# Expert layer of a streaming-encoder block: index casts on another engine, a reduction over adjacent elements, and the last eight chunks' activations computed first

## The chip, the cores and the metric

The kernel runs on one core of a Trainium2 chip. The metric is the device time of one execution in microseconds. The time before the change is the median of three runs, 1779.57 us (1777.91 to 1783.63). The core's engines are TensorE (PE, matrix products), VectorE (DVE), ScalarE (ACT), GpSimd (POOL) and SyncE (SP, which here only issues DMAs). Each takes its instructions strictly in program order and waits on semaphores for the others, so an instruction that waits holds up everything behind it on its engine.

## The reference, cut to what matters

The block takes 512 tokens of 1024 channels. It computes chunked attention beside a diagonal state-space mixer, then cross-attention into 256 memory tokens, then an expert layer with 16384 single-neuron experts. The change touches only the expert layer:

```python
def _peer_ffn(hn, w_q, sub_keys, u_tab, v_tab):
    def block(xb):                                   # 128 tokens
        q = (xb @ w_q).reshape(PEER_BLOCK, PEER_HEADS, 2, PEER_QDIM // 2)
        s = jnp.einsum('thsd,hsnd->thsn', q, sub_keys).astype(jnp.float32)
        sv, si = lax.top_k(s, PEER_TOPK)             # 16 of 128, twice
        cand = (sv[:, :, 0, :, None] + sv[:, :, 1, None, :]).reshape(PEER_BLOCK, PEER_HEADS, -1)
        cidx = (si[:, :, 0, :, None] * PEER_KEYS + si[:, :, 1, None, :]).reshape(PEER_BLOCK, PEER_HEADS, -1)
        top, pos = lax.top_k(cand, PEER_TOPK)        # 16 of the 256 sums
        e = jnp.take_along_axis(cidx, pos, axis=-1)
        g = jax.nn.softmax(top, axis=-1)
        act = jax.nn.gelu(jnp.einsum('thkd,td->thk', u_tab[e], xb), approximate=False)
        w = (g * act).astype(xb.dtype)
        return jnp.einsum('thk,thkd->td', w, v_tab[e])
```

There are 8 heads, two key halves each, and 16 experts for each token and head.

## The kernel before

The 512 tokens are four blocks of 128. For one block (block 0) the expert rows are gathered from memory by index, 128 gathers from each table. For the other three blocks (384 tokens, `NT`) the kernel computes **all** 16384 experts densely, in 128 chunks of 128 experts, and multiplies the activations by a gate table that is zero where an expert was not chosen.

The expert layer has these stages.

1. *Queries and top-k.* `queries(h)` computes a head's scores on PE; ACT evacuates them (`pqT`, `sc`, `scl`). `topk(h, scs, g)` finds the 16 best on DVE: group 0 takes two token blocks, groups 1 and 2 one block each. It finds the best 16 of each half (`tv`, `ti`), casts the indices to floats and scales the first half's by 128 (`tf`, lines 890 and 891), adds 54 candidate pairs (`ca` on DVE, `cx` on POOL, line 898), finds the best 16 of those (`top`, `pi`), casts these positions to bf16 (`pf`, line 912), and picks the expert numbers out: `eq` on DVE compares a table of positions with `pf` (line 917), POOL multiplies `eq` by `cx` into `ev` (line 918), and DVE sums `ev` over the 54 candidates (line 919). `ev` has one buffer and is stored candidate by candidate, 16 numbers each, so the sum reads one element in 16. Group 0 of all heads and group 1 of heads 0 to 5 run in this stage.
2. *First U chunks.* A U chunk (`u_steps`) is one SP load of 512 KB (`wraw`), a split into a rounded half `whi` (ACT, line 108) and a rest `wlo` (line 110; POOL for the first `FREE` = 12 chunks, DVE for all later ones), 24 matmuls into `pa` (lines 124 to 126) and a Gelu on ACT into a tile `act` (line 1050). Chunks 0 to 11 are written behind the top-k.
3. *Gate table.* `build_w` makes the table in 48 quads of 8 tokens: DVE builds one-hot tables (`oAE`, line 1019, once; `oB`, line 1023, twice), PE multiplies them (`pw`, line 1028), ACT evacuates (`stg`, line 1031) and SP stores to `Wd` in memory. The generator yields 96 times, after every 8 `pw` matmuls. Between these steps stand the U chunks 12 to 27 (`FREE` to `LEAD` = 28), in pieces of 6 matmuls, and group 1 of heads 6 and 7.
4. *Main loop.* Iteration n computes U chunk n + 28 (while there is one) and V chunk n (`v_phase`): a load and a split of a V chunk, `act` times its gates `wt` (DVE, line 1074; `wt` is loaded from `Wd` by ACT's DMA queue), the split of the product (`ah` on ACT, line 1076, `al` on DVE, line 1080) and 18 matmuls into six accumulators `acc` (line 1084) that live through the whole loop. The 256 gathers (POOL) and their products (DVE) are spread over the iterations from n = 11 on; group 2 of the top-k stands in iterations 1 to 8. The last 28 iterations have V chunks only.

The order on each engine is made by a scheduler when the kernel is built, from the order of the code, the priorities that `tc.issue_after` sets, and a model of the instructions' lengths. The activations live in a ring of 31 tiles.

Of the kernel before, what the change touches and what calls it, by code (L numbers as in the profile page):

```python
# [800 lines left out]

NT = 384
LEAD = 28
FREE = 12
HOLD = 10
IOH = 2
ULV = (8,)
KS = 2
H0 = 2
SLACK = 4  # L810
# [9 lines left out]
def peer(tc, I, c, out):  # L820
# [5 lines left out]
    with tc.tile_pool(name="pp", bufs=1) as pp, tc.tile_pool(name="tq", bufs=2) as tq:  # L826
# [50 lines left out]
        def topk(h, scs, g):  # L877
            nb, b0 = len(scs[0]), (0, 2, 3)[g]
            tv = tq.tile([128, 2, nb, 16], F32, tag="tv", name="tv")
            ti = tq.tile([128, 2, nb, 16], U32, tag="ti", name="ti")  # L880
            for s in range(2):
                for b in range(nb):
                    sb = scs[s][b]
                    V.max(tv[:, s, b, 0:8], sb)
                    V.max_index(ti[:, s, b, 0:8], tv[:, s, b, 0:8], sb)
                    V.match_replace(sb, tv[:, s, b, 0:8], sb, NEG_BIG)
                    V.max(tv[:, s, b, 8:16], sb)
                    V.max_index(ti[:, s, b, 8:16], tv[:, s, b, 8:16], sb)
            tf = tq.tile([128, 2, nb, 16], F32, tag="tf", name="tf")
            V.tensor_copy(tf, ti)  # L890
            V.tensor_scalar(tf[:, 0], tf[:, 0], 128.0, None, op0=OP.mult)
            ca = tq.tile([128, nb, NC_], F32, tag="ca", name="ca")
            cx = tq.tile([128, nb, NC_], F32, tag="cx", name="cx")
            o = 0
            for i0, n, w_ in ROWS:
                for src, dst in ((tv, ca), (tf, cx)):
                    sh = [128, nb, n, w_]
                    (V if dst is ca else G).tensor_tensor(  # L898
                        dst[:, :, o:o + n * w_].rearrange("p b (n w) -> p b n w", n=n),
                        src[:, 0, :, i0:i0 + n].unsqueeze(3).broadcast_to(sh),  # L900
                        src[:, 1, :, 0:w_].unsqueeze(2).broadcast_to(sh), op=OP.add)
                o += n * w_
            pi = tq.tile([128, nb, 16], U32, tag="pi", name="pi")
            pf = tq.tile([128, nb, 16], BF16, tag="pf", name="pf")
            for b in range(nb):
                cb, tb = ca[:, b], top[:, b0 + b, h]
                V.max(tb[:, 0:8], cb)
                V.max_index(pi[:, b, 0:8], tb[:, 0:8], cb)
                V.match_replace(cb, tb[:, 0:8], cb, NEG_BIG)
                V.max(tb[:, 8:16], cb)  # L910
                V.max_index(pi[:, b, 8:16], tb[:, 8:16], cb)
            V.tensor_copy(pf, pi)
            for b in range(nb):
                sh = [128, NC_, 16]
                eq = tq.tile(sh, BF16, tag="eq", name="eq")
                ev = pp.tile(sh, F32, tag="ev", name="ev", bufs=1)
                V.tensor_tensor(eq, iob, pf[:, b].unsqueeze(1).broadcast_to(sh), op=OP.is_equal)
                G.tensor_tensor(ev, eq, cx[:, b].unsqueeze(2).broadcast_to(sh), op=OP.mult)
                V.tensor_reduce(ex[:, b0 + b, h], ev.rearrange("p n k -> p k n"), axis=AX.X, op=OP.add)  # L919

        def gates(g):
            r = ((0, 2), (2, 3), (3, 4))[g]
# [116 lines left out]
        acts = {}  # L1039
        wts = {}  # L1040

        def u_steps(n):
            w = load_split(I["ut"][n], G if n < FREE else V)
            pa = pst("s", "pa")[:, :NT]
            for k in range(8):
                mm3(pa, [t[:, k] for t in w], [PTh(k)[:, 128:], PTl(k)[:, 128:]], k == 0, k == 7)
                if k < 7 and (k + 1) % KS == 0:
                    yield
            acts[n] = act_tile("act")
            S.activation(acts[n], pa, AF.Gelu)  # L1050
            yield

        def u_phase(n):
            for _ in u_steps(n):
                pass
# [7 lines left out]
        def v_phase(n):  # L1063
# [13 lines left out]
            if n % 4 == WTP and n + 4 < 128:  # L1077
                with tc.issue_after(c.ah_ins):
                    load_wt(n // 4 + 1)
            c.v_ins = V.tensor_tensor(al, a, ah, op=OP.subtract).ins  # L1080
            for b in range(3):
                for (l, r) in ((ah, 0), (ah, 1), (al, 0)):
# [7 lines left out]
        prepare(1)  # L1090
        for n in range(FREE):
            u_phase(n)
        steps = (None for n in range(FREE, LEAD) for _ in u_steps(n))
        done = 0
        for q in range(96):
            next(gw)
            if q in LATE:
                i = LATE.index(q)
                with tc.issue_after(c.w_ins):
                    gates(1) if i == H0 else topk_late(8 - H0 + i, 1)  # L1100
            with tc.issue_after(c.pw_ins):
                while done < (q + 1) * (8 // KS) * (LEAD - FREE) // 96:
                    next(steps)
                    done += 1
        for _ in gw:
# [1 line left out]
        due = 0  # L1107
        res = []
        for n in range(128):
            if n + LEAD < 128:  # L1110
                u_phase(n + LEAD)
            v_phase(n)
            if 1 <= n < 9:
                with tc.issue_after(c.v_ins):
# [6 lines left out]
                        res.append(s8([128, 2, 1024], "res"))  # L1121
                        nc.scalar.dma_start(res[i][:, :2 - i], h2[1 + 2 * i:3 + i].rearrange("b p d -> p b d"))
            if n > HOLD:
                due += 256 * (2 if n + LEAD < 128 else 1) / (256 - LEAD - 2 * HOLD - SLACK)
            while due >= 1:
                due -= 1
                with tc.issue_after(c.split_ins):
# [78 lines left out]
```

## Time and profile before

| | |
|---|---|
| median of three runs | 1779.57 us |
| the profiled execution | 1780.63 us |
| its span, first to last instruction | 1778.9 us |
| mean granted PE clock | 0.977 |
| PE busy / DVE busy / ACT busy / POOL busy | 1682.0 / 1398.8 / 717.6 / 689.5 us |
| HBM read / written | 348.72 / 32.51 MB |

The page gives the busy time of each engine over the whole span and in 40 equal slices, the chain of work that ended last, and groups of instructions by line. Further views used below are the windows (one row for a stretch of time: busy time and instruction count of each engine, granted PE clock, DMA share and rate), the groups of one stretch kept apart by shape, the waits (who waited for whom: total, times, longest), and the timeline (start, length, engine, line, operation). A busy time of an instruction can cover the end of the one before it, since the engines pipeline; how far two instructions of one kind stand apart is read from their starts.

### The profile page before, as it was taken

How to read it: one execution, taken by the hardware profiler on the slowest of the kernel's cores; microseconds unless marked ns; L12 is line 12 of the kernel's file. 1: busy time of each engine (PE TensorE's matmuls, PEld its weight loads, DVE VectorE, ACT ScalarE, POOL GpSimd, SP SyncE). 2: the span in 40 equal slices, each digit the busy share in tenths (PEclk: the TensorE clock that was granted, in tenths of full speed). 3: DMA queues.
4: the chain of work that ended last, by engine and by line, in shares of the span. 5: the costliest groups of instructions: out<-in, count | busy, mean ns of one | idle time of the engine just before them, and what ended most of it. 6: DMA issues, size and time to landing. Idle time of an engine off the chain costs nothing.

```text
span 1778.9 us, 24797 instructions
## 1 busy us (share of the span) xinstructions
PE 1682.0 (95%) x8929; PEld 1462.1 (82%) x8929; DVE 1398.8 (79%) x2755; ACT 717.6 (40%) x1161; POOL 689.5 (39%) x566
## 2 busy tenths in 40 slices
PE   7898999999999668899999999999999999999999
PEld 6676778877788667788888999999999999999887
DVE  7998563644589999995998787777777877777886
ACT  4242573432333227785333333333333333333332
POOL 5432232341466651200345444444343434334451
PEclk9998999999999889999999999999999999999999
DMA  5412323220422226786449998888888888888895
GB/s 189 115 55 89 113 101 142 95 83 15 175 92 81 66 72 208 213 238 225 163 151 352 331 334 303 308 313 303 306 315 293 331 311 318 297 315 300 324 366 212
DMA packets 155820, 383.19 MB, mean 215 GB/s; under 512 B 13993, under 2 KB 70825, under 8 KB 155569
## 3 DMA queue, kind: packets, MB, share of 16 engines
q1 hardware_dynamic: 107504, 212.83, 35.1%
q0 software_dynamic: 36864, 134.23, 21.1%
q10 hardware_dynamic: 11328, 34.54, 5.5%
q8 instruction: 70, 1.15, 0.2%
q14 instruction: 54, 0.43, 0.1%
HBM read 348.72 MB, written 32.51 MB: 214 GB/s over the span
## 4 chain that ended last, share of the span: by engine, by line
PE 71%; DVE 22%; issue 3%; DMA 2%; POOL 1%; ACT 1%; SPq 0%; DVEq 0%; ACTq 0%; POOLq 0%
PE acc L1084 27%; PE pa L124 8%; PE pa L126 8%; PE pa L125 8%; PE pv L124 3%; PE pv L126 3%; PE pv L125 3%; DVE oB L1023 2%; DVE oAE L1019 2%; DVE ex L919 2%; DVE wlo L110 2%; PE pS L684 1%; PE po L694 1%; DVE ca L898 1%; PE pw L1028 1%
## 5 line engine op out<-in xcount | busy, mean ns | idle before, releaser
L108 ACT ACTIVATE whi<-wraw 128x1024 fp32r<-128x1024 f32 (+1 forms) x332 | 349.7, 1055 | 486.9 <-PE pa L125 229.9
L124 PE MATMUL pa<-PTh,whi 128*128 128x384 f32 x1024 | 355.8, 347 | 21.9 <-ACT act L1050 18.2
L126 PE MATMUL pa<-PTh,wlo 128*128 128x384 f32 x1024 | 350.5, 342 | 14.2 <-POOL wlo L110 10.8
L110 DVE TENSOR_TENSOR wlo<-wraw,whi 128x1024 fp32r<-128x1024 f32 x262 | 321.1, 1226 | 53.4 <-ACT whi L108 53.1
L125 PE MATMUL pa<-PTl,whi 128*128 128x384 f32 x1024 | 349.4, 341 | 0.0
L972 POOL DMA_INDIRECT vg<-in_peer_v_dram,ei x128 | 182.1, 1423 | 240.0 <-DVE X L973 216.7
L962 POOL DMA_INDIRECT ug<-in_peer_u_dram,ei x128 | 177.5, 1386 | 225.2 <-DVE ug L963 201.0
L1084 PE MATMUL acc<-wlo,ah 128*128 128x512 f32 x768 | 238.6, 392 | 0.8 <-DVE wlo L110 0.8
L1084 PE MATMUL acc<-whi,ah 128*128 128x512 f32 x768 | 239.2, 392 | 0.0
L1084 PE MATMUL acc<-whi,al 128*128 128x512 f32 x768 | 237.3, 391 | 0.0
L124 PEld LDWEIGHTS pa<-PTh,whi 128*128 128x128 f32 x1024 | 196.6, 192 | 28.1 <-ACT act L1050 20.3
L110 POOL TENSOR_TENSOR wlo<-wraw,whi 128x1024 fp32r<-128x1024 f32 x70 | 170.2, 2441 | 126.7 <-ACT whi L108 126.6
L126 PEld LDWEIGHTS pa<-PTh,wlo 128*128 128x128 f32 x1024 | 196.8, 192 | 17.2 <-POOL wlo L110 12.4
L125 PEld LDWEIGHTS pa<-PTl,whi 128*128 128x128 f32 x1024 | 196.7, 192 | 3.8
L973 DVE SCALAR_TENSOR_TENSOR X<-vg,dots,X 128x1024 f32<-128x1024 f32 x128 | 164.5, 1285 | 16.3 <-DMA vg<-in_peer_v_dram,ei 10.4
L1076 ACT ACTIVATE ah<-act 128x384 fp32r<-128x384 f32 x128 | 67.1, 526 | 260.7 <-PE acc L1084 241.5
L1084 PEld LDWEIGHTS acc<-wlo,ah 128*128 128x128 f32 x768 | 144.6, 188 | 33.3 <-DVE wlo L110 1.5
L1084 PEld LDWEIGHTS acc<-whi,al 128*128 128x128 f32 x768 | 144.1, 188 | 30.9
L963 DVE SCALAR_TENSOR_TENSOR ug<-ug,X 128x1024 f32<-128x1024 f32 x128 | 151.9, 1222 | 20.6 <-DMA ug<-in_peer_u_dram,ei 20.5
L1084 PEld LDWEIGHTS acc<-whi,ah 128*128 128x128 f32 x768 | 143.2, 188 | 23.7
L1080 DVE TENSOR_TENSOR al<-act,ah 128x384 fp32r<-128x384 f32 x128 | 70.9, 555 | 58.7 <-ACT ah L1076 56.3
L1074 DVE TENSOR_TENSOR act<-act,wt 128x384 f32<-128x384 f32 x128 | 66.0, 576 | 58.3 <-DMA wt<-Wd 58.3
(383 smaller groups left out, 2721.9 us busy)
## 6 DMA issues: line engine op xcount, KB each, us to landing
wraw<-in_ut_dram SPq DMA_DIRECT2D x128, 512.0 KB, 5.0
wraw<-in_peer_v_dram SPq DMA_DIRECT2D x128, 512.0 KB, 5.5
Wd<-stg SPq DMA_DIRECT2D x24, 1024.0 KB, 6.5
wt<-Wd ACTq DMA_DIRECT2D x32, 768.0 KB, 7.9
wraw<-in_w_pq_dram SPq DMA_DIRECT2D x16, 512.0 KB, 3.3
h<-in_x_dram SPq DMA_DIRECT2D x8, 512.0 KB, 7.2
wraw<-in_w_qk_dram SPq DMA_DIRECT2D x8, 512.0 KB, 3.7
wraw<-in_w_mk_dram SPq DMA_DIRECT2D x8, 512.0 KB, 3.3
```

The source lines that it names most:

```text
L108: S.activation(hi, raw, AF.Copy)
L110: ins = leng.tensor_tensor(lo, raw, hi, op=OP.subtract).ins
L124: P.matmul(out, lhs[0], rhs[0], start=first, stop=False)
L125: P.matmul(out, lhs[0], rhs[1], start=False, stop=False)
L126: P.matmul(out, lhs[1], rhs[0], start=False, stop=last)
L962: G.indirect_dma_start(out=ug, out_offset=None, in_=I["peer_u"], in_offset=IOX(ap=ei[:, k:k + 1], axis=0))
L963: V.scalar_tensor_tensor(ug, ug, 1.0, c.X0, op0=OP.mult, op1=OP.mult, accum_out=dots[:, k:k + 1])
L972: G.indirect_dma_start(out=vg, out_offset=None, in_=I["peer_v"], in_offset=IOX(ap=ei[:, k:k + 1], axis=0))
L973: V.scalar_tensor_tensor(a0, vg, dots[:, k:k + 1], a0, op0=OP.mult, op1=OP.add)
L1076: c.ah_ins = S.activation(ah, a, AF.Copy).ins
L1080: c.v_ins = V.tensor_tensor(al, a, ah, op=OP.subtract).ins
L1084: P.matmul(acc[b * 2 + d], l[:, b * 128:(b + 1) * 128], v[r][:, d * 512:(d + 1) * 512], start=n == 0 and l is ah and r == 0, stop=n == 127 ...
```

## The change

Three things are edited. The casts of the top-k indices and positions become ACT instructions. `ev` is stored the other way round, the 54 candidates of one result beside each other, so POOL writes with a stride and DVE's sum reads adjacent elements. And the U chunks are computed in another order: chunks 120 to 127 first (`NSPILL` = 8), then 0 to 119. The first eight activations are stored to memory (`Ad`) by ACT's DMA queue and loaded back by it in the iterations n = 117 to 124, three iterations ahead of their use. The gate table now has 24 U chunks spread over it (16 before), the main loop computes U chunk number n + 36 in its order, which is chunk n + 28, until n = 91, and the last 36 iterations have V chunks only.

```diff
 LEAD = 28
+NSPILL = 8
...
             tf = tq.tile([128, 2, nb, 16], F32, tag="tf", name="tf")
-            V.tensor_copy(tf, ti)
-            V.tensor_scalar(tf[:, 0], tf[:, 0], 128.0, None, op0=OP.mult)
+            S.activation(tf[:, 0], ti[:, 0], AF.Copy, scale=128.0)
+            S.activation(tf[:, 1], ti[:, 1], AF.Copy)
...
-            V.tensor_copy(pf, pi)
+            S.activation(pf, pi, AF.Copy)
             for b in range(nb):
                 sh = [128, NC_, 16]
                 eq = tq.tile(sh, BF16, tag="eq", name="eq")
-                ev = pp.tile(sh, F32, tag="ev", name="ev", bufs=1)
+                ev = pp.tile([128, 16, NC_], F32, tag="ev", name="ev", bufs=1)
                 V.tensor_tensor(eq, iob, pf[:, b].unsqueeze(1).broadcast_to(sh), op=OP.is_equal)
-                G.tensor_tensor(ev, eq, cx[:, b].unsqueeze(2).broadcast_to(sh), op=OP.mult)
-                V.tensor_reduce(ex[:, b0 + b, h], ev.rearrange("p n k -> p k n"), axis=AX.X, op=OP.add)
+                G.tensor_tensor(ev.rearrange("p k n -> p n k"), eq, cx[:, b].unsqueeze(2).broadcast_to(sh), op=OP.mult)
+                V.tensor_reduce(ex[:, b0 + b, h], ev, axis=AX.X, op=OP.add)
...
-        def u_steps(n):
-            w = load_split(I["ut"][n], G if n < FREE else V)
+        UORDER = [*range(128 - NSPILL, 128), *range(128 - NSPILL)]
+        Ad = c.dr.tile([NSPILL, 128, NT], F32, name="Ad")
+
+        def u_steps(j):
+            n = UORDER[j]
+            w = load_split(I["ut"][n], G if j < FREE else V)
...
-            acts[n] = act_tile("act")
-            S.activation(acts[n], pa, AF.Gelu)
+            a = act_tile("act")
+            S.activation(a, pa, AF.Gelu)
+            if j < NSPILL:
+                nc.scalar.dma_start(Ad[j], a)
+            else:
+                acts[n] = a
             yield
...
+            if 0 <= n + 3 - (128 - NSPILL) < NSPILL:
+                with tc.issue_after(c.ah_ins):
+                    acts[n + 3] = act_tile("act")
+                    nc.scalar.dma_start(acts[n + 3], Ad[n + 3 - (128 - NSPILL)])
...
-        steps = (None for n in range(FREE, LEAD) for _ in u_steps(n))
+        steps = (None for n in range(FREE, LEAD + NSPILL) for _ in u_steps(n))
...
-                while done < (q + 1) * (8 // KS) * (LEAD - FREE) // 96:
+                while done < (q + 1) * (8 // KS) * (LEAD + NSPILL - FREE) // 96:
...
-            if n + LEAD < 128:
-                u_phase(n + LEAD)
+            if n + LEAD + NSPILL < 128:
+                u_phase(n + LEAD + NSPILL)
...
-                due += 256 * (2 if n + LEAD < 128 else 1) / (256 - LEAD - 2 * HOLD - SLACK)
+                due += 256 * (2 if n + LEAD + NSPILL < 128 else 1) / (256 - LEAD - NSPILL - 2 * HOLD - SLACK)
```

The scheduler's order moves with it. In the top-k stage, ACT's program before the change holds only score evacuations, splits and query evacuations (here the last two heads; `scl` are the late groups' scores):

```order
L108 ACTIVATE whi<-wraw 128x1024
L861 ACTIVATE pqT<-ppq 128x512
L108 ACTIVATE whi<-wraw 128x1024
L861 ACTIVATE pqT<-ppq 128x512
L865 ACTIVATE sc<-ppS 128x256
L870 ACTIVATE scl<-ppS 128x128 x2
```

The same place of ACT's program in the changed kernel (line numbers are one higher; 891 and 892 are the `tf` casts, 913 the `pf` cast, x16 columns for groups 1 and 2, x32 for group 0):

```order
L108 ACTIVATE whi<-wraw 128x1024
L862 ACTIVATE pqT<-ppq 128x512
L913 ACTIVATE pf<-pi 128x32
L866 ACTIVATE sc<-ppS 128x256
L871 ACTIVATE scl<-ppS 128x128 x2
L891 ACTIVATE tf<-ti 128x32
L913 ACTIVATE pf<-pi 128x16
L891 ACTIVATE tf<-ti 128x16
L892 ACTIVATE tf<-ti 128x16
L866 ACTIVATE sc<-ppS 128x256
L871 ACTIVATE scl<-ppS 128x128 x2
```

The casts now stand between one head's evacuations and the next, so ACT waits there for DVE's indices, with the next `sc` behind them.

In the gate table, ACT's program before has one U chunk (a `whi` and an `act`) for every 12 evacuations `stg`; the rows are from the middle of the stage, where the gates of group 1 (`top`) are exponentiated:

```order
L1031 ACTIVATE stg<-pw 128x4x64 x12
L108 ACTIVATE whi<-wraw 128x1024
L1050 ACTIVATE act<-pa 128x384
L1031 ACTIVATE stg<-pw 128x4x64 x10
L927 ACT_TABLE_LOAD
L927 ACTIVATE top<-top 128x128
L1031 ACTIVATE stg<-pw 128x4x64 x2
```

The same engine and place in the changed kernel:

```order
L1032 ACTIVATE stg<-pw 128x4x64 x2
L913 ACTIVATE pf<-pi 128x16
L1032 ACTIVATE stg<-pw 128x4x64 x6
L108 ACTIVATE whi<-wraw 128x1024
L1056 ACTIVATE act<-pa 128x384
L928 ACT_TABLE_LOAD
L928 ACTIVATE top<-top 128x128
L1032 ACTIVATE stg<-pw 128x4x64 x8
```

One U chunk now stands behind every 8 evacuations. On PE this is 594 `pa` matmuls between the first and the last `pw`, against 420; on SP the chunks' loads stand among the `Wd` stores in the same proportion.

Near the end of the main loop ACT's program of the changed kernel reads, for the iterations n = 117 and after (`Ad` are the stored activations, `act` their tiles; the two `res` loads just ahead of these rows stood there before as well):

```order
L1071 DMA wt<-Wd 128x1536
L1093 DMA act<-Ad 128x384
L108 ACTIVATE whi<-wraw 128x1024
L1086 ACTIVATE ah<-act 128x384
L1093 DMA act<-Ad 128x384
```

One load of 192 KB was added to each of eight iterations there.

## The prediction

> **What bounds the kernel now.** First the page: busy share of each engine, and PE, DVE and PE's granted clock in 40 slices of 44.5 us.
>
> ```profile
> PE 1682.0 (95%) x8929; PEld 1462.1 (82%) x8929; DVE 1398.8 (79%) x2755; ACT 717.6 (40%) x1161; POOL 689.5 (39%) x566
> ...
> PE   7898999999999668899999999999999999999999
> ...
> DVE  7998563644589999995998787777777877777886
> ...
> PEclk9998999999999889999999999999999999999999
> ```
>
> PE is full except around slices 13 to 18, where DVE is full instead. So I cut the time there by stage: top-k, the end of top-k with the first U chunks, gate table, start of the main loop, its U and V part, its V part.
>
> ```profile
> 489.00:534.00 45.00, 45.00 (x228) 38.24 (x227) 38.51 (x222) 15.73 (x37) 30.46 (x34) 1.00 0.26 91
> 534.00:657.00 123.00, 91.26 (x455) 81.24 (x453) 121.11 (x476) 33.60 (x63) 79.56 (x84) 0.90 0.23 74
> 657.00:818.00 161.00, 143.62 (x1240) 129.27 (x1240) 153.69 (x251) 122.98 (x230) 19.56 (x12) 0.94 0.71 210
> 818.00:987.00 169.00, 160.40 (x785) 143.13 (x784) 147.87 (x404) 60.69 (x85) 63.44 (x73) 0.98 0.65 228
> 987.00:1656.00 669.00, 669.00 (x3387) 609.47 (x3386) 514.86 (x641) 239.98 (x329) 278.57 (x205) 1.00 0.87 312
> ```
>
> The columns are PE, PE's weight loads, DVE, ACT, POOL, granted clock, DMA share, GB/s. From 534 to 657 DVE works 121.1 of 123 us and PE only 91.3, at a clock of 0.90; from 657 to 818 DVE works 153.7 of 161. After that PE sets the pace. The chain of waits confirms it for the main loop:
>
> ```profile
> 1000.03 4.12 PE acc L1084 x18
> ...
> 1647.95 4.12 PE acc L1084 x18
> ...
> 1656.26 118.15 PE acc L1084 x521
> ```
>
> From 1000.03 to 1647.95 lie 78 pairs of a U and a V chunk: 647.92 / 78 = 8.307 us each. Alone, V chunks take 118.15 / 521 x 18 = 4.08 us. So **a U chunk costs the main loop 4.22 us of PE, and nothing there hides it.**
>
> **The change, term by term.**
>
> *C, the main loop.* The order shows 78 + 2136 `pa` matmuls behind the last `pw`, against 62 + 2326: 174 fewer, 7.25 U chunks. 7.25 x 4.22 = **30.6 us less**. The 8 V chunks that lose their U partner still take 4.08 us. There DMA is the next limit:
>
> ```profile
> 1723.00:1756.00 33.00, 33.00 (x147) 27.35 (x146) 28.13 (x34) 12.27 (x16) 13.56 (x8) 1.00 0.94 362
> ...
> ACT whi L108 <- DMA wraw<-in_peer_v_dram: 11.8, 8, 3.4
> ```
>
> V chunks alone already move 362 GB/s at a share of 0.94 (so about 385 at full share), and ACT waits 8 times for their weights, yet the PE chain does not break. A V chunk moves 524 kB of weights (512 KB on the page), 197 kB of `wt` and, with 256 / 196 instead of 256 / 204 gathers a unit, 685 kB of gathered rows: 1.41 MB, 3.7 us at 385 GB/s, under 4.08. Only the last ten chunks also carry the `res` loads and the reloads, 3.1 MB together, 8 us of DMA against 10 x 0.4 us of room. Bounds 0 to 4 us; I take **+2**, since three `wraw` buffers run ahead. The new wait, of DVE's `act` product for the reload, has `al` and the next `wlo` behind it; the load is issued three chunks (12 us) ahead, and the 768 KB `wt` loads land in 7.9 us:
>
> ```profile
> wt<-Wd ACTq DMA_DIRECT2D x32, 768.0 KB, 7.9
> ```
>
> So it costs nothing unless landing exceeds 12 us. The eight stores stand on ACT's queue in the top-k stage, where ACT is busy 33.6 of 123 us.
>
> *A, the top-k.* DVE from 534 to 657:
>
> ```profile
> L919 DVE TENSOR_REDUCE ex<-ev 128x16 f32<-128x864 f32 x17 | 27.9, 1640 | 1.5 <-POOL ev L918 1.5
> ...
> L898 DVE TENSOR_TENSOR ca<-tv 128x8 f32<-128x8 f32 x10 | 7.4, 735 | 0.0
> ...
> L912 DVE CAST pf<-pi 128x16 bf16<-128x16 uint32 x5 | 4.6, 923 | 0.0
> ...
> L890 DVE CAST tf<-ti 128x64 f32<-128x64 uint32 x5 | 3.1, 622 | 0.0
> ...
> L891 DVE TENSOR_SCALAR tf<-tf 128x16 f32<-128x16 f32 x5 | 3.0, 591 | 0.0
> ...
> L890 DVE CAST tf<-ti 128x32 f32<-128x32 uint32 x16 | 2.8, 172 | 0.0
> ```
>
> The strided sum takes 1640 ns. A sum of adjacent elements, and the cost of one more element on DVE, are in these rows:
>
> ```profile
> L928 DVE TENSOR_REDUCE gs<-top 128x16 f32<-128x256 f32 x1 | 0.4, 415 | 0.0
> L1023 DVE TENSOR_TENSOR oB<-oAE,gp 128x1024 f16<-128x1024 f16 x96 | 61.7, 698 | 0.0
> L1019 DVE TENSOR_TENSOR oAE<-ioz,iT 128x2048 f16<-128x2048 f16 x48 | 59.9, 1259 | 0.0
> L110 DVE TENSOR_TENSOR wlo<-wraw,whi 128x1024 fp32r<-128x1024 f32 x19 | 23.4, 1229 | 0.0
> L1080 DVE TENSOR_TENSOR al<-act,ah 128x384 fp32r<-128x384 f32 x14 | 7.6, 547 | 2.0 <-PE acc L1084 2.0
> ```
>
> (1229 - 547) / 640 = 1.07 ns an element, so 864 adjacent ones take 415 + 608 x 1.07 = 1.06 us: 0.58 less, x17 = 9.9 us. The three casts shown hold 10.7 us of DVE. Most of that is a wait for POOL to finish its instruction:
>
> ```profile
> 597.33 1.98 POOL L918 TENSOR_TENSOR ev<-eq,cx 128x864 f32<-128x864 bf16 x1 [3.02 <-DVE eq L917]
> 597.69 1.65 DVE L912 CAST pf<-pi 128x16 bf16<-128x16 uint32 x1
> ```
>
> The cast ends at 599.34, POOL's product at 599.31. Where POOL does not hold it, such a cast takes some 0.17 us (the last row above), so 15 of them hold about 2.5 us of work and 8 of waiting. The `ca` adds wait in the same way (735 ns for 8 elements), so a part of the 8 will be waited for by the next of them; I take half. Sum: 9.9 + 2.5 + 4 = **16 us less**; bounds 10 and 21 where nothing else turns up, and 0 by the rivals. [...]
>
> What is late next: POOL with 79.6 of 123 us and PE with 91.3 still fit into 107, and PE's clock should rise from 0.90. On ACT a cast costs about what a 16-column Gelu of `dots` does:
>
> ```profile
> L966 ACT ACTIVATE dots<-dots 128x16 f32<-128x16 f32 x8 | 1.7, 214 | 10.6 <-DVE ug L963 10.6
> ```
>
> *B, the gate table.* PE's step of 8 `pw` and 6 `pa`, by starts:
>
> ```profile
> 768.59 0.65 PE L1028 MATMUL pw<-oB,oAE 128*128 128x128 f16 x8
> 769.04 0.42 PE L124 MATMUL pa<-PTh,whi 128*128 128x384 f32 x1
> 769.30 0.34 PE L125 MATMUL pa<-PTl,whi 128*128 128x384 f32 x1
> ...
> L1028 PE MATMUL pw<-oB,oAE x768: 217/218/330, 666.2 to 817.6; 128*128 128x128 f16 x192
> ```
>
> 8 `pw` take 0.45 us, the first `pa` behind them 0.26, the others 0.174 ((1656.26 - 1652.07) / 24 in the chain above). Now: 96 x 0.45 + 420 x 0.174 + 65 x 0.09 = 122 us of the 151.4 between the first and the last `pw`. After: 96 x 0.45 + 594 x 0.174 + 96 x 0.09 = 155. DVE after: 153.7 + 7.25 splits x 1.23 - 3 sums x 0.58 - about 1 for casts = 160. So the stage, set by DVE alone now, gets two engines at 155 to 160 us. DVE's 6 us more are the floor; PE, now without slack, loses a little whenever DVE turns to the top-k of heads 6 and 7, which stands in this stage. I take **+9**; the upper bound is the moved work laid end to end, 30. Each moved chunk also brings two ACT instructions and a load:
>
> ```profile
> L108 ACT ACTIVATE whi<-wraw 128x1024 fp32r<-128x1024 f32 x18 | 19.1, 1064 | 13.8 <-issue 9.8 <-PE pa L125 4.0
> L1050 ACT ACTIVATE act<-pa 128x384 f32<-128x384 f32 x18 | 8.6, 476 | 0.0
> ```
>
> ACT grows from 123.0 by 7.25 x 1.54 to 134 of 161 us, DMA share from 0.71 to 0.79 (3.8 MB more on 210 GB/s x 161 us = 33.8); neither is late. On SP the loads now stand among the `Wd` stores, which wait for ACT; three buffers put them two chunks (12 us) ahead of their use. POOL's 12 splits stay 12.
>
> **Sum**, against the profiled execution's 1780.63: -30.6 + 2 - 16 + 9 = -35.6, 1745. That execution is 1.06 above the median 1779.57, so **1744**.
>
> **Rivals.** *R1, ACT hands the gain back.* The casts stand in ACT's program behind splits that wait for their load:
>
> ```profile
> ACT whi L108 <- DMA wraw<-in_ut_dram: 34.5, 5, 11.5
> ...
> L110 POOL TENSOR_TENSOR wlo<-wraw,whi 128x1024 fp32r<-128x1024 f32 x17 | 40.5, 2387 | 0.0
> L918 POOL TENSOR_TENSOR ev<-eq,cx 128x864 f32<-128x864 bf16 x17 | 32.1, 1890 | 35.7 <-DVE ex L919 27.0 <-DVE eq L917 8.2 <-DVE tf L891 0.6
> ```
>
> Five such waits, 6.9 us on average. If two or three fall between DVE's index and its cast, A is gone: 1760. Against it: those loads wait for POOL, which waits 27 us for DVE's sums, so a faster DVE shortens them. Chance 0.17.
>
> *R2, POOL's strided write.* The sum's stride of 64 bytes costs DVE 1640 against 1060 ns; POOL now writes at steps of 216 bytes. At the same ratio `ev` goes from 1.89 to 2.92 us, 17.5 us over 17 products with one buffer: A is eaten, 1761. Chance 0.08. [...] POOL's own adjacent products of 1024 elements take 2.39 us, no less per element than `ev`, so its arithmetic may hide the write, and I leave it at nothing.
>
> *R3, the refill does not fit:* B at +30, 1765. PE's idle time in the stage speaks against it. Chance 0.08. *R4, the V part becomes DMA's:* C's +2 becomes +8, 1750; chance 0.04. *R5, slower:* R2's mechanism at a greater price. The products lie in a chain with one buffer, so what each grows by shows 17 times; from +2.1 us (twice today's time) all 36 us are gone, and at +2.7 the time is 1790. Chance 0.04. *R6, nothing measurable:* R1 and R3 together, 1779; chance 0.02.
>
> **How the numbers follow.** My forecast, every term near its value, has 0.57. A measurement of this kernel tells about 0.3% (5.3 us) from no change. Faster by more than that: forecast, R1 to R4, 0.94; same 0.02; slower 0.04. The range: down to 1730 with A at -21, B at +4 and C at -31; up to 1764, which takes in R1, R2 and R4 and half of R3.
>
> **What would show it.** Right: 36 V chunks of about 4.08 us at the end; the sum near 1.06 us; first `pw` near 650; last `pw` near 811 (817.6 now). Wrong in A: DVE idle behind ACT's `pf` or `tf`, or `ev` above 2.5 us. Wrong in B: more than 165 us from first to last `pw`. Wrong in C: gaps in the `acc` chain behind loads of `wraw` or `Ad`.

## The result, and the profile after

| | before | after |
|---|---|---|
| median of 4 runs | 1779.52 us | 1737.04 us |
| lowest and highest | 1777.91, 1783.63 | 1736.26, 1737.83 |
| ratio to before, 95% interval | | 0.9758 [0.9741, 0.9775] |
| span of the profiled execution | 1778.9 us | 1735.8 us |
| start to first `pw` (top-k) | 666.2 us | 651.6 us (-14.6; forecast -16) |
| first to last `pw` (gate table) | 151.4 us | 165.8 us (+14.4; forecast +9) |
| last `pw` to end (main loop) | 961.3 us | 918.4 us (-42.9; forecast -28.6) |

The changed kernel is 42.5 us faster where 35.6 were forecast. The sum hides errors of opposite sign (the loop gained 14.3 us more than forecast, the gate table lost 5.4 more), so each stage has to be read. First the page after, with the same rows as before: busy times, then PE, DVE and PE's granted clock in 40 slices (43.4 us each now).

```profile
PE 1670.2 (96%) x8929; PEld 1451.0 (84%) x8929; DVE 1364.0 (79%) x2683; ACT 731.9 (42%) x1233; POOL 709.5 (41%) x566
...
PE   7898999999999789989999999999999999999999
...
DVE  7998564645569989986997887777777787788987
...
PEclk9997999999999989999999999999999999999999
```

The hole in PE at slices 13 to 18 has become shallow, and DVE has given up some of its nines there. Next the windows of the kernel after: top-k, gate table, the first 170 us of the main loop, V chunks alone. The columns are as before: PE, weight loads, DVE, ACT, POOL, clock, DMA share, GB/s.

```profile
489.00:651.00 162.00, 143.17 (x725) 127.12 (x724) 148.59 (x669) 57.58 (x143) 112.90 (x117) 0.96 0.29 95
651.00:818.00 167.00, 160.45 (x1373) 143.84 (x1372) 150.72 (x238) 136.20 (x250) 27.87 (x12) 0.98 0.76 224
...
818.00:988.00 170.00, 168.64 (x854) 153.20 (x853) 145.45 (x390) 68.04 (x115) 69.25 (x77) 1.00 0.71 253
...
1580.00:1735.00 155.00, 151.55 (x670) 125.20 (x668) 126.55 (x149) 52.38 (x69) 63.08 (x40) 1.00 0.86 325
```

In the gate table PE is now the fuller engine (160.45 of 167, DVE 150.72), and from 818 on PE is busy nearly without a break. The end of the chain of waits (its last row) and the row of the `pw` matmuls:

```profile
1580.55 150.79 PE acc L1098 x665
```
```profile
L1029 PE MATMUL pw<-oB,oAE x768: 217/218/330, 651.6 to 817.4; 128*128 128x128 f16 x192
```

The V part is one unbroken chain: 150.79 / 665 x 18 = 4.08 us a chunk, as before the change. So the 2 us set aside for DMA did not come. The reloads were waited for once, by DVE and for 2.1 us, and PE did not notice.

### The profile page after: what moved, and what is told of

It is laid out like the page before. It is cut to its first block, busy times and chain, and to the rows that moved or that the text cites. A ratio compares the mean times of both kernels' runs of the same rounds, so it can differ in the third digit from the quotient of the medians.

```text
span 1735.8 us, 24849 instructions
## 1 busy us (share of the span) xinstructions
PE 1670.2 (96%) x8929; PEld 1451.0 (84%) x8929; DVE 1364.0 (79%) x2683; ACT 731.9 (42%) x1233; POOL 709.5 (41%) x566
## 3 DMA queue, kind: packets, MB, share of 16 engines
q1 hardware_dynamic: 107504, 212.83, 36.7%
## 4 chain that ended last, share of the span: by engine, by line
PE 73%; DVE 19%; DMA 3%; issue 3%; POOL 2%; ACT 1%; ACTq 0%; DVEq 0%; SPq 0%; POOLq 0%
PE acc L1098 27%; PE pa L124 9%; PE pa L126 8%; PE pa L125 8%; PE pv L124 2%; PE pw L1029 2%; PE pv L126 2%; PE pv L125 2%; DVE wlo L110 2%; DVE ca L899 1%; DVE ex L920 1%; PE pS L684 1%; DVE xn L175 1%; DMA ug<-in_peer_u_dram,ei 1%; PE pmo L774 1%
## 5 line engine op out<-in xcount | busy, mean ns | idle before, releaser
L126 PE MATMUL pa<-PTh,wlo 128*128 128x384 f32 x1024 | 347.0, 339 | 0.0
L963 POOL DMA_INDIRECT ug<-in_peer_u_dram,ei x128 | 184.0, 1437 | 205.6 <-DVE ug L964 182.2
L899 POOL TENSOR_TENSOR cx<-tf 128x8 f32<-128x8 f32 (+6 forms) x120 | 44.1, 403 | 175.3 <-ACT tf L892 175.0
L1032 ACT ACTIVATE stg<-pw 128x256 f32<-128x256 f32 x192 | 104.1, 682 | 27.0 <-PE pw L1029 21.4
```

The source lines that it names most:

```text
L126: P.matmul(out, lhs[1], rhs[0], start=False, stop=last)
L963: G.indirect_dma_start(out=ug, out_offset=None, in_=I["peer_u"], in_offset=IOX(ap=ei[:, k:k + 1], axis=0))
L1032: S.activation(stg[e][:, :, q * 8 + hf * 4:q * 8 + hf * 4 + 4].rearrange("p i t -> p t i"), pw.rearrange("p (t i) -> p t i", t=4)[:, :, e ...
```

## The experiments

All whole times below are medians of four runs; the stages are read from each kernel's one profiled execution.

| kernel | first `tv` | first `pw` | gate table | loop | median | ratio to before, 95% interval |
|---|---|---|---|---|---|---|
| before | 489.4 | 666.2 | 151.4 | 961.3 | 1779.52 | |
| changed | 489.6 | 651.6 | 165.8 | 918.4 | 1737.04 | 0.9758 [0.9741, 0.9775] |
| e1, top-k edits only | 490.2 | 651.8 | 144.2 | 955.7 | 1753.66 | 0.9859 [0.9843, 0.9876] |
| e2, parked chunks only | 489.6 | 666.2 | 167.2 | 924.6 | 1759.87 | 0.9892 [0.9875, 0.9908] |
| e3, casts back on VectorE | 486.5 | 657.8 | 161.3 | 920.1 | 1745.21 | 0.9814 [0.9797, 0.9830] |
| e8, strided sums back | 486.0 | 651.7 | 168.5 | 922.8 | 1745.66 | 0.9806 [0.9788, 0.9823] |
| e4, later transposes | 491.1 | 652.7 | 165.7 | 917.6 | 1735.08 | 0.9752 [0.9736, 0.9768] |
| e5, half the splits on GpSimd | 489.6 | 650.9 | 167.0 | 918.2 | 1737.84 | 0.9759 [0.9743, 0.9775] |
| e6, twelve parked | 488.6 | 649.8 | 171.6 | 911.1 | 1735.04 | 0.9744 [0.9727, 0.9761] |
| e7, as e5 with ten parked | 489.9 | 652.2 | 171.3 | 912.6 | 1735.26 | 0.9745 [0.9729, 0.9762] |
| e9, front-loaded table | 488.2 | 648.9 | 161.2 | 918.5 | 1731.07 | 0.9719 [0.9701, 0.9736] |
| e10, twelve parked, early reload | 488.4 | 650.0 | 171.6 | 905.9 | 1728.16 | 0.9702 [0.9684, 0.9720] |
| e11, as e10, gathers moved | 489.8 | 651.4 | 171.6 | 906.8 | 1731.49 | 0.9719 [0.9702, 0.9737] |

The first `tv` is where DVE's top-k begins. It lies between 486.0 and 491.1 us although no edit touches the stages ahead of it, where every engine has the same instructions in the same order. So the length from first `tv` to first `pw` is to be compared, not the place of the first `pw`.

### e1 and e2: where the main loop's extra 12 us come from

The loop gained 42.9 us; 7.25 chunks at 4.22 us are 30.6. The two kernels split the change in its halves. e1 parks nothing:

```diff
-NSPILL = 8
+NSPILL = 0
-        Ad = c.dr.tile([NSPILL, 128, NT], F32, name="Ad")
```

> The change without its parked chunks: casts on ScalarE and adjacent sums as in the changed kernel, all U chunks in the old order. Two theories of why the main loop gained 42.9 us (last pw to end 961.3 -> 918.4) where 7.25 chunks x 4.22 us are 30.6. T1, the group-2 top-k at the loop's start: a shorter DVE there no longer holds PE back; it belongs to the top-k part. Then this kernel has it: last pw to end about 949, first pw about 651.6, gate table about 148, in all about 1750 us. T2, the step from gate table to loop: more pa matmuls behind the last pw cover the wait for wt, and PE's clock does not fall after it; it belongs to the moved chunks. Then this kernel does not have it: last pw to end about 961, in all about 1762 us.

e2 keeps the parked chunks and has the old casts and the strided sum:

```diff
-            S.activation(pf, pi, AF.Copy)
+            V.tensor_copy(pf, pi)
...
-                ev = pp.tile([128, 16, NC_], F32, tag="ev", name="ev", bufs=1)
+                ev = pp.tile(sh, F32, tag="ev", name="ev", bufs=1)
...
-                G.tensor_tensor(ev.rearrange("p k n -> p n k"), eq, cx[:, b].unsqueeze(2).broadcast_to(sh), op=OP.mult)
+                G.tensor_tensor(ev, eq, cx[:, b].unsqueeze(2).broadcast_to(sh), op=OP.mult)
-                V.tensor_reduce(ex[:, b0 + b, h], ev, axis=AX.X, op=OP.add)
+                V.tensor_reduce(ex[:, b0 + b, h], ev.rearrange("p n k -> p k n"), axis=AX.X, op=OP.add)
```

> The parked chunks alone, with the old casts and strided sums. T1 (the loop's extra 12 us belong to the shorter group-2 top-k): last pw to end about 931, gate table 151.4 + 16, in all about 1765 us. T2 (they belong to the step from gate table to loop): last pw to end about 918, in all about 1753 us. Both: first pw near 666, the sum near 1640 ns.

Measured: e1's loop is 5.6 us shorter than before's, e2's 36.7 us, that is 6.1 more than the moved chunks. e1's loop also holds 18 `pa` matmuls more than before's (2406 behind the last `pw`, 2388 before; its table has 402 instead of 420), 3.1 us of PE, so counted in the same way it gained 8.7. (Its table took 144.2 us, 7.2 less than before, with these 18 fewer; with the parked chunks beside the top-k edits, and 594 `pa` in both, it is 1.4, 165.8 against e2's 167.2.) Both theories expected one of the two to have all 12 and the other none, so **each holds in part**. That 8.7 and 6.1 are more together than the 12.3 fits the cover at the step into the loop, which is in both (below). The windows of the first 170 us of the loop show what was gained, first before, then e1, then e2; the changed kernel's stands above:

```profile
818.00:988.00 170.00, 161.40 (x790) 144.05 (x789) 148.87 (x406) 61.21 (x86) 64.44 (x73) 0.98 0.65 228
```
```profile
796.00:966.00 170.00, 165.54 (x841) 150.13 (x839) 143.11 (x386) 66.61 (x113) 68.03 (x74) 1.00 0.71 246
```
```profile
834.00:1004.00 170.00, 164.55 (x825) 149.22 (x824) 150.11 (x411) 62.45 (x87) 65.42 (x75) 0.99 0.68 239
```

Before, PE stood idle for 8.6 of these 170 us at a clock of 0.98; in the changed kernel for 1.4 at 1.00. That is 7.2 us of waiting, and two hundredths of 170 us, 3.4: 10.6 of the 12.3 (the remaining 1.7 I can't place). The waits of PE in these windows, of before, e1 and e2 (engine and what it waited for: us in total, times, longest):

```profile
PE pa L124 <- ACT whi L108: 3.7, 1, 3.7
PE pa L126 <- DVE wlo L110: 3.4, 3, 1.5
PE acc L1084 <- DVE wlo L110: 0.8, 1, 0.8
...
```
```profile
PE pa L126 <- DVE wlo L110: 2.3, 2, 1.7
PE acc L1097 <- ACT ah L1085: 2.1, 1, 2.1
```
```profile
PE pa L126 <- DVE wlo L110: 3.3, 2, 2.8
PE acc L1098 <- DVE wlo L110: 1.5, 1, 1.5
PE acc L1098 <- ACT ah L1086: 0.6, 1, 0.6
```

PE's wait at the step from the table to the loop was 3.7 us (for ACT's `whi`); it is 2.1 in e1 and 0.6 in e2 (for `ah`). In both, 78 `pa` matmuls stand there ahead of the first `acc`, 62 before: the scheduler moved some from the table to this place whichever half of the change it was given, so this cover is not the parking's own, as T2 had it. The waits for DVE's `wlo` stay with the parked chunks alone (4.2 us before, 4.8). They fall (to 2.3) where the top-k of block 0, which DVE does in iterations 1 to 8, has become shorter. The changed kernel has both, and is left with 1.0 and 0.4 us.

### e3 and e8: the parts of the top-k

e3 puts the casts back on DVE and keeps the adjacent sums:

```diff
-            S.activation(tf[:, 0], ti[:, 0], AF.Copy, scale=128.0)
-            S.activation(tf[:, 1], ti[:, 1], AF.Copy)
+            V.tensor_copy(tf, ti)
+            V.tensor_scalar(tf[:, 0], tf[:, 0], 128.0, None, op0=OP.mult)
...
-            S.activation(pf, pi, AF.Copy)
+            V.tensor_copy(pf, pi)
```

> The changed kernel with its casts back on VectorE, sums adjacent, chunks parked. If the prediction's split of the top-k term holds (2.5 us of work and 4 of waiting for POOL belong to the casts): first pw about 658, in all about 1744 us. If the waits for POOL all come back elsewhere whoever casts: first pw about 654, in all about 1740. If the casts on ScalarE are the whole gain and the sums none: first pw about 662, about 1748.

e8 keeps the casts on ACT and undoes the sums' layout (the three lines on `ev` of e2's diff):

> The changed kernel with GpSimd writing ev in rows as before and VectorE summing at a stride, casts on ScalarE, chunks parked. By the prediction the sums are 9.9 of the 16 us of the top-k term (17 x 0.58): first pw about 661, and in all, with the sums behind the table, about 1749 us. If GpSimd's strided write (2.32 us against 1.89 to 2.06) has taken back part of it: first pw about 656, in all about 1743. If the casts alone made the gain: first pw 652, 1737.

The two profiled executions reached the top-k earlier than the changed kernel's, e3's by 3.1 us and e8's by 3.6. Here is e8's first `tv` (486.0), then the changed kernel's:

```profile
L885 DVE MAX8 tv<-sc x48: 265/276/304, 486.0 to 904.0; 128x8 f32<-128x128 f32 x48
```
```profile
L885 DVE MAX8 tv<-sc x48: 267/276/296, 489.6 to 898.6; 128x8 f32<-128x128 f32 x48
```

From the first `tv` to the first `pw`, with the parked chunks in all four, it is 176.6 us (neither edit: e2), 171.3 (sums alone: e3), **165.7 (casts alone: e8)** and 162.0 (both). The eight other kernels with both edits take 160.7 to 162.3. So up to the gate table the casts alone bring 10.9 us and the sums 3.7 on top of them, where the forecast gave the sums 9.9 of 16. The first `pw` itself, 651.7 in e8 and 651.6 in the changed kernel, would have said that the sums bring nothing. e3 prices less: one U chunk more stands ahead of its first `pw` (288 `pa` matmuls and 22 of DVE's splits, 264 and 19 in the other three), which makes its top-k look longer and its gate table, at 161.3 us, shorter. So its 657.8 and 1745.21 us, though close to the first expectation (658 and 1744), do not show the predicted split to be right.

In the whole time both count: undoing the casts costs 8.2 us (e3's four runs spread from 1740.97 to 1747.18, and the one profiled is the fastest), undoing the sums 8.6. In e8's stages the sums cost 3.7 us in the top-k, 2.7 in the gate table and 4.4 in the loop, less the 3.6 of its earlier start. With the changed kernel's start its first `pw` would stand at 655.3, near the second expectation (656), but not for the reason given there: POOL's strided write costs too little (R2 below). Where the sums' gain before the table went, DVE's groups show. Three each, from 534 us to the first `pw`: before, e8, and the changed kernel (count | busy us, mean ns | idle time ahead of them):

```profile
L919 DVE TENSOR_REDUCE ex<-ev 128x16 f32<-128x864 f32 x18 | 29.5, 1641 | 1.5 <-POOL ev L918 1.5
L898 DVE TENSOR_TENSOR ca<-tv 128x16 f32<-128x16 f32 (+6 forms) x50 | 15.7, 360 | 0.0
L917 DVE TENSOR_TENSOR eq<-iob,pf 128x864 bf16<-128x864 bf16 x16 | 11.9, 756 | 0.0
```
```profile
L920 DVE TENSOR_REDUCE ex<-ev 128x16 f32<-128x864 f32 x17 | 27.9, 1639 | 3.9 <-POOL ev L919 3.9
L899 DVE TENSOR_TENSOR ca<-tv 128x16 f32<-128x16 f32 (+6 forms) x50 | 16.6, 384 | 0.0
...
L918 DVE TENSOR_TENSOR eq<-iob,pf 128x864 bf16<-128x864 bf16 x16 | 13.0, 833 | 0.0
```
```profile
L899 DVE TENSOR_TENSOR ca<-tv 128x16 f32<-128x16 f32 (+6 forms) x50 | 19.5, 442 | 0.0
L920 DVE TENSOR_REDUCE ex<-ev 128x16 f32<-128x864 f32 x18 | 18.6, 1036 | 4.4 <-POOL ev L919 4.4
L918 DVE TENSOR_TENSOR eq<-iob,pf 128x864 bf16<-128x864 bf16 x16 | 15.4, 979 | 0.0
```

The sum takes 1036 ns (forecast 1.06 us). But the shorter DVE gets, the longer its additions `ca` and comparisons `eq` become, with the same counts and shapes: from before to e8 `ca` 0.9 us, `eq` 1.1 and the wait for `ev` 2.4, together 4.4 of the casts' 13.6 us (their rows stand further below); from e8 to the changed kernel `ca` 2.9, `eq` 2.4 and the wait 0.5, together 5.8. The sums gave 9.3 us in these rows, and 10.9 for 18 against 18: at 534 us e8 is 2.9 us further on in its program, so one of its sums lies ahead of the window. Two `oB` more, 1.4 us, stand ahead of the changed kernel's first `pw`; what is left of the 10.9 is about the 3.7 that the stage shows. That fits the waits for POOL of which the prediction spoke: from 534 us to the first `pw`, each of the six casts of over 1.2 us before the change ends 0.03 to 0.05 us after a POOL instruction, and each of the ten `ca` of over 0.7 us in the changed kernel ends within 0.11 us of the end of one. Taken off one instruction, a part of the wait came up at others.

### e4, e5, e9: what the gate table's 5 us more are

In the changed kernel PE waits once for long in the gate table. Its timeline (start, length, what it waited for), and the windows around:

```profile
746.52 0.34 PE L126 MATMUL pa<-PTh,wlo 128*128 128x384 f32 x1
752.23 0.45 PE L991 MATMUL wtp<-ident,f 128*128 128x128 f32 x1 [5.37 <-DVE f L988]
...
754.08 0.52 PE L126 MATMUL pa<-PTh,wlo 128*128 128x384 f32 x1
754.40 0.52 PE L124 MATMUL pa<-PTh,whi 128*128 128x384 f32 x1
```
```profile
651.00:731.00 80.00, 79.44 (x686) 71.49 (x685) 78.24 (x146) 67.04 (x126) 25.08 (x12) 1.00 0.76 224
731.00:751.00 20.00, 15.24 (x129) 13.12 (x127) 20.00 (x27) 16.14 (x29) 2.79 (x1) 0.99 0.77 228
751.00:771.00 20.00, 18.77 (x145) 16.92 (x146) 15.28 (x24) 13.05 (x24) 0.00 (x0) 0.84 0.52 152
771.00:818.00 47.00, 47.00 (x418) 42.32 (x416) 37.20 (x44) 39.97 (x74) 0.00 (x0) 1.00 0.86 254
```

PE reaches the transposes (`wtp`) for the table's third block at 746.9 and waits 5.4 us for rows that DVE computes (line 988). Behind the wait its matmuls start 0.32 us apart instead of 0.174, until 757.4: the clock is 0.84 from 751 to 771, 3.2 us more. Together 8.6: here some five slow microseconds (752.2 to 757.4) stand behind 5.4 idle ones.

e4 asks whether the place of the transposes is the cause. The rows are computed earlier, into the buffer of `ev` instead of the one that they shared with the row before, and the transposes stand two quarter-steps later:

```diff
-PREP = (1, 3)
+PREP = (1, 3, 2)
+PREPF = (1, 2)
...
-                    if (b, sb) == PREP:
-                        prepare(2)
+                    if (b, sb) == PREPF:
+                        early = prepare_f(2)
...
                     for q in range(4):
+                        if (b, sb, q) == PREP:
+                            prepare(2, early)
```

> The changed kernel, with the index rows of the third block computed in a buffer of their own one sub-block earlier, and their three transposes two quarter-steps later in PE's program, so that PE does not reach the first transpose before VectorE has its rows. Theory B1: the gate table's 14.4 us instead of 9 are that one wait (PE 5.4 us for the row f) and the slower matmuls behind it (clock 0.91 in that stretch): first to last pw about 158 instead of 165.8, in all about 1730 us. Rival B2: the stage is PE's work alone, the wait is only a place where slack shows: first to last pw about 165, in all about 1737.

Measured 165.7 us for the table, and 2 us less in the median (the two kernels' runs overlap): B1 falls. The wait only changed its name. These are PE's waits in e4's gate table, and the window where most of them lie:

```profile
PE pw L1039 <- DVE oB L1034: 5.8, 7, 3.2
```
```profile
752.00:772.00 20.00, 15.38 (x111) 13.62 (x109) 17.01 (x24) 11.21 (x20) 0.00 (x0) 0.83 0.89 254
```

So it is not the transposes but DVE, which is full up to there. e5 takes work from it:

```diff
-            w = load_split(I["ut"][n], G if j < FREE else V)
+            w = load_split(I["ut"][n], G if j < FREE or (j < LEAD + NSPILL and j % 2) else V)
```

> The changed kernel with every other U chunk of the gate table split on GpSimd (12 of 24; 2.4 us each there) and not on VectorE (1.23 us each). Theory D, from the run with the later transposes, where PE's wait only moved: VectorE's work up to about 755 us sets the first part of the gate table, and PE's work sets only the rest; 14.8 us less on VectorE then takes away the wait (5.4 us) and the low clock behind it (about 3): first to last pw about 157 instead of 165.8, in all about 1729 us. Rival: the two engines share what they lose, GpSimd's splits come late or hold VectorE, and PE waits for wlo instead: first to last pw 165 or more, in all 1737 or more.

The table took 167.0 us: the rival's outcome. But DVE did not get any shorter, so theory D was not tested. DVE's `oB` and POOL's splits in the gate table, first of the changed kernel, then of e5:

```profile
L1024 DVE TENSOR_TENSOR oB<-oAE,gp 128x1024 f16<-128x1024 f16 x95 | 60.9, 682 | 4.0 <-PE wtp L992 4.0
```
```profile
L1024 DVE TENSOR_TENSOR oB<-oAE,gp 128x1024 f16<-128x1024 f16 x96 | 81.8, 894 | 0.4
...
L110 POOL TENSOR_TENSOR wlo<-wraw,whi 128x1024 fp32r<-128x1024 f32 x12 | 64.7, 5398 | 64.2 <-ACT whi L108 64.2
```

A split that took POOL 2.39 us beside the top-k (the prediction's row) takes it 5.40 beside DVE's products, and these take 894 instead of 682 ns: 20.9 us more on DVE, where 14.8 were to be saved. DVE's busy time in the stage rose from 150.7 to 162.4 us. e7 does the same with two chunks more:

```diff
-NSPILL = 8
-FREE = 12
+NSPILL = 10
+FREE = 14
```

> As the run with every other split on GpSimd, with two chunks more parked, and two more U chunks ahead of the table with their splits on GpSimd. If VectorE was what held the stage (theory D), PE alone is left, and moving two chunks more is worth nothing (8.35 us of PE in the stage against 8.4 us in the loop) except where PE idles: the time of that run or up to 5 us less, about 1724 to 1729. If D falls: 1737 or more.

Its 1735.26 us lie between the two expectations; as DVE is no shorter there either (162.5 us busy), it says nothing of D.

e9 tests D without POOL. It moves one chunk's matmuls and split from behind the point where PE ran dry to ahead of it:

```diff
-                while done < (q + 1) * (8 // KS) * (LEAD + NSPILL - FREE) // 96:
+                while done < ((q + 1) * 15 // 14 if q < 56 else 60 + (q - 55) * 9 // 10):
```

> The changed kernel, with the 24 U chunks of the gate table not spread evenly: 15 of them in its first 56 of 96 steps and 9 in the other 40, where it was 14 and 10. Theory D, as the run with twelve parked chunks leaves it: VectorE sets the stage up to the third block's transposes (752 us), and PE runs dry there; PE sets the rest. One chunk moved to the front then costs VectorE 1.2 us ahead of that point, and saves PE 4.2 us behind it, and PE does not run dry, so its clock stays up: first to last pw about 160 instead of 165.8, in all about 1731 us. Rival: the stage has the same length wherever PE's work stands in it, as it had with later transposes: 165 to 167, about 1737 us.

Measured: table 161.2 us, time **1731.07 us**, as D expects. PE's long wait has shrunk from 5.4 to 3.1 us, and the clock of the stage is 0.99:

```profile
648.00:810.00 162.00, 158.31 (x1370) 142.80 (x1369) 151.76 (x239) 134.93 (x249) 27.22 (x12) 0.99 0.77 230
```

In the profiled execution 2.7 us more lie before the first `pw`, which D doesn't explain: 1.4 of them ahead of the first `tv`, the other 1.3 in the top-k, which takes 160.7 us here and 161.2 to 162.3 in the other kernels with both top-k edits.

### e6, e10, e11: how far parking carries

```diff
-NSPILL = 8
+NSPILL = 12
```

> Twelve chunks parked, not eight. If PE's work sets the gate table, the four chunks (96 matmuls x 0.174 = 16.7 us) come back there and go from the loop (3.75 x 4.22 = 15.8 us): gate table about 182, in all about 1737 us, no change. If there is slack left in the stage (PE idle 6.6 us, clock below full for 3 us): gate table about 174, in all about 1729. If VectorE sets it: its 4 splits are 4.9 us, gate table about 171, in all about 1727. If the memory traffic of the longer V part becomes the bound: gaps in the acc chain, above 1740.

The gate table with four chunks more is only 5.8 us longer, and in it PE never waits:

```profile
649.00:821.00 172.00, 172.00 (x1454) 156.58 (x1453) 157.87 (x243) 141.26 (x257) 20.08 (x12) 1.00 0.77 229
```

Between the first and the last `pw` stand 90 `pa` matmuls more than in the changed kernel (684 against 594). Of their 15.7 us 9.9 went into slack: the wait of 5.4 us, the small ones of 1.2 and the 3.2 of the slow clock. The length, 171.6 us, is the one expected if VectorE sets the stage (171), but a PE that never waits doesn't bear that out. It supports D from the other side: with more work per step PE arrives at the transposes after DVE. But the loop became only 7.3 us shorter where 15.8 were due. Of the 8.5 missing some 4 lie in its first 170 us, where PE is busy for 166.29 us at a clock of 0.99 (168.64 at 1.00 in the changed kernel), and the rest at its end. The chain there, and the reloads' time from issue to landing:

```profile
1556.32 113.84 PE acc L1098 x502
1670.62 20.46 DMA act<-Ad
...
1697.63 27.74 PE acc L1098 x120
```
```profile
DMA to landing us min/median/max: 6.1/9.6/20.5
```

Three iterations ahead (12 us) was too late here, where the DMAs already moved 381 GB/s (1640 to 1670 us). e10 reloads twelve ahead, when the U chunks have ended and tiles are free:

```diff
+AHEAD = 12
...
-            if 0 <= n + 3 - (128 - NSPILL) < NSPILL:
+            if 0 <= n + AHEAD - (128 - NSPILL) < NSPILL:
                 with tc.issue_after(c.ah_ins):
-                    acts[n + 3] = act_tile("act")
-                    nc.scalar.dma_start(acts[n + 3], Ad[n + 3 - (128 - NSPILL)])
+                    acts[n + AHEAD] = act_tile("act")
+                    nc.scalar.dma_start(acts[n + AHEAD], Ad[n + AHEAD - (128 - NSPILL)])
```

> Twelve chunks parked, and each reloaded twelve chunks ahead of its use, not three. With three, twelve reloads cost the end of the loop: one landed after 20.5 us, VectorE waited 10.5 us for them, and the acc chain broke once; by the count of its matmuls the V part took 169.05 us where 40.9 chunks take 167. If the late reload is why twelve gain only 2 us: no wait for the reload, an unbroken acc chain, about 1733 us. If the traffic itself is the limit (381 GB/s there), the wait goes over to the weights or the gathered rows: about 1735, no change.

Measured **1728.16 us**, the fastest kernel here. The chain is whole again, 165.30 / 729 x 18 = 4.08 us a chunk:

```profile
1555.01 165.30 PE acc L1099 x729
```

The gain over e6 is 6.9 us, more than the 2 expected; its loop is 5.2 us shorter. From the last `pa` matmul to the end, where the reloads count, it takes 172.8 us, e6 176.5: 3.7 of the 5.2. The other 1.5 lie in the pairs, and no run tells why. e11 also takes a quarter of the gathers out of the V part:

```diff
-                due += 256 * (2 if n + LEAD + NSPILL < 128 else 1) / (256 - LEAD - NSPILL - 2 * HOLD - SLACK)
+                due += 256 * (2 if n + LEAD + NSPILL < 128 else 0.75) / (256 - LEAD - NSPILL - 2 * HOLD - SLACK - 0.25 * (LEAD + NSPILL))
```

> As the run before it, and the gathers moved out of the V part: a V chunk without a U partner takes 0.75 shares of them instead of 1, the pairs take the rest. If traffic in the V part is the limit, this lowers it (about 1.2 instead of 1.4 MB a chunk) and the end runs at PE's pace: about 1732 us. If the pairs have no room for it (318 GB/s at a share of 0.89), gaps come into the pairs: above 1737.

1731.49 us is 3.3 more than e10. In the profiled executions it is 2.3: the first `tv` comes 1.4 us later, the pairs take 1.8 more, and the V part 0.9 less. With early reloads the V part is nearly PE's already, and there is little left to relieve.

## Why the prediction was right, and where not

The likeliest case came true, with 1737 where 1744 was forecast; of the signs set out for it, the V chunks of 4.08 us, the sum and the first `pw` came as written, and the last `pw` came at 817.4 instead of 811. A sign of being wrong came too: more than 165 us from first to last `pw`, 165.8. That the time fell so close is in part luck. The loop gained 42.9 us, more than the 31 that the range allowed for it at most, and the larger loss in the gate table took back more than a third of that error. The terms, by size of the error:

- **C, the main loop, was mis-sized: -28.6 forecast, -42.9 measured.** The 30.6 us for 7.25 chunks are right and the +2 for DMA was too cautious. What failed is that the step counted only PE's instructions. The prediction's own window of 818 to 987 us showed PE busy for 160.40 of 169 us at a clock of 0.98, and gave these idle 8.6 us no term. They went almost entirely, in part with the parked chunks (above all the wait at the step into the loop), in part with the top-k edits, whose eight sums for block 0 the prediction had not followed into the loop.
- **B, the gate table, was mis-sized: +9 forecast, +14.4 measured.** PE's work was counted right: 165.8 less the 5.4 and 1.2 us that it waited for DVE and 3.2 for the clock is 156, forecast 155. The step took the larger of two averages over the whole stage, DVE 160 and PE 155, and they were of different stretches: DVE's was counted from 657 us on, 9 us ahead of the first `pw`. From the first `pw` on DVE worked 144.69 us before the change:

```profile
666.00:818.00 152.00, 134.62 (x1196) 120.37 (x1195) 144.69 (x238) 121.55 (x228) 19.56 (x12) 0.94 0.74 219
```

  With the same additions that gives 151, and 150.72 were measured, so by averages PE's 155 was the larger and the stage would have grown by 4 us. No average holds the rest, the waits and the clock. In truth the stage has two halves: DVE is full up to about 752 us, because the top-k of heads 6 and 7 stands there, and PE from then on. (PE keeps up for most of the first half, 79.44 us of the first 80, and runs dry at its end.) What PE loses in the first half isn't made up in the second. e9 and e6 show this; e4 shows that it doesn't hang on the transposes.
- **A, the top-k, came as forecast (-14.6 for -16), but its parts did not,** so here too luck had a part. DVE lost 24.5 us of instructions before the first `pw`: 10.9 of sums and the casts' 13.6, which these three groups of before hold:

```profile
L912 DVE CAST pf<-pi 128x32 bf16<-128x32 uint32 (+1 forms) x10 | 6.5, 652 | 0.0
L890 DVE CAST tf<-ti 128x64 f32<-128x64 uint32 (+1 forms) x10 | 3.6, 394 | 0.0
L891 DVE TENSOR_SCALAR tf<-tf 128x32 f32<-128x32 f32 (+1 forms) x10 | 3.5, 378 | 0.0
```

  It got back 3.8 us in `ca`, 3.5 in `eq` and 2.9 in the wait for `ev`: 14.3 are left. The forecast let half of the casts' waiting for POOL come back at the adds, 4 us. With the casts alone gone (e8) `ca` grew by 0.9 us, `eq` by 1.1 and the wait for `ev` by 2.4; the rest of the growth came with the sums, from which the forecast let nothing come back. So the casts were sized too small (10.9 us for 6.5, also because all their rows hold 13.6 us and the prediction counted 10.7, of the longest ones) and the sums too large (3.7 on top of the casts for 9.9).
- **R1 did not come.** ACT waits for no load in this stretch any more. Its longest waits from 534 to 651 us are now the casts' own, for DVE, and DVE waits for no cast there (0.7 us in all ahead of it):

```profile
ACT tf L892 <- DVE ti L889: 25.1, 7, 6.7
ACT pf L913 <- DVE pi L912: 24.0, 6, 7.1
```

- **R2 and R5 did not come.** POOL's strided write costs some 0.15 us an instruction, not 1.03. Here `ev` before the first `pw` in before and after (e8, with casts on ACT and `ev` written in rows, has 1844 ns):

```profile
L918 POOL TENSOR_TENSOR ev<-eq,cx 128x864 f32<-128x864 bf16 x22 | 41.2, 1871 | 39.6 <-DVE ex L919 27.0 <-DVE eq L917 12.0 <-DVE tf L891 0.6
```
```profile
L919 POOL TENSOR_TENSOR ev<-eq,cx 128x864 f32<-128x864 bf16 x22 | 44.2, 2011 | 25.7 <-DVE ex L920 16.4 <-DVE eq L918 9.3
```

- **R3 did not come with eight chunks** (14.4, not 30), nor with twelve. **R4** did not come with eight; with twelve its mechanism appears, through the reloads (e6), and goes away when they are issued earlier (e10). **R6** did not come.

## What to carry to other kernels

Where an engine sets the pace of a stretch, its idle time and its lowered clock there belong in the sum as much as its instructions: a change elsewhere can collect them (here 7.2 us of waiting and 3.4 of clock in the first 170 us of the loop). Two engines that are both near full in a stage are to be compared over parts of the stage, not by their totals; work moved in should land where the engine that takes it runs dry (e9: 161.2 us for the table instead of 165.8). Time taken off DVE, whose long casts and additions ended with POOL's instructions, was not all saved here; a part came back in `ca`, `eq` and the wait for `ev` (4.4 of 13.6 us with the casts, 5.8 of 10.9 with the sums). And stages of two single executions are compared from the same event in the program, not from the start of the run.

## What was not expected of the hardware

- DVE's f16 products and POOL's splits both took longer in one stage: POOL's split went from 2.39 to 5.40 us, DVE's product from 682 to 894 ns (e5). Twelve splits moved off DVE made it busier, 162.4 us for 150.7.
- A wait of 5.4 us on PE cost about 3 us more by the clock behind it (0.84 from 751 to 771 us, changed kernel).
- A reload of 192 KB that lands in 9.6 us at the median took up to 20.5 us where the DMAs moved 381 GB/s (e6).
